# FFN weight low parts: an adding transfer on GpSimd's queue in place of a VectorE subtraction

## The chip, the cores and the metric

One core of one Trainium2 chip. The metric is the device time of one execution in microseconds (us). The kernel before takes 1315.03 us, the median of three runs (1314.34 to 1315.76). About 0.2% (2.6 us) is what a measurement of this kernel can tell from no change.

## The reference

A two-layer trunk on 512 tokens of width 1024, in float32. Layer 0 is a gated linear recurrence (HGRN2) and a SwiGLU FFN; then one shared K/V is projected; layer 1 is band attention and a second FFN. Every sub-layer has an RMSNorm, a shift and scale from a conditioning vector, and a gate on the residual. What the change touches are weights of the two FFNs:

```python
def swiglu(u, w_in, w_out):                     # w_in 1024 x 5632, w_out 2816 x 1024
    gate, up = jnp.split(u @ w_in, 2, axis=-1)
    return (jax.nn.silu(gate) * up) @ w_out
...
u = modulate(rms_norm(h, norm_ffn[layer]), sh2, sc2)
h = h + g2[:, None, :] * swiglu(u, ffn_w_in[layer], ffn_w_out[layer])
```

## The kernel before, in words

Activations lie as [features, tokens]: 8 tiles `h[j]` of 128 x 512. Every weight matrix comes in chunks of 128 x (8 x 128) float32 (512 KB; the third chunk of each FFN output tile has 6 blocks, 384 KB). `weight_plan` lists all chunks in the order in which TensorE uses them.

A float32 product is made of three products in the faster type float32r: value = high part + low part, and w x u is taken as high x high, high x low and low x high (`mm3`, L161, L162, L163; L163 is the one that uses a weight's low part). So each chunk is split (`split`): ScalarE copies the raw chunk into `wh`, rounded to float32r (L115), and VectorE subtracts, `wl = raw - wh` (L116). A chunk gives 24 products of 512 columns (18 in a third chunk).

`raw`, `wh` and `wl` each have three buffers (pool `wp`, bufs=3). So chunk i+3 can be split when TensorE has left chunk i. SyncE's queue (SP) issues the loads, and a raw buffer is free once both halves of the split have read it.

The program is recorded through a scheduler, which sets the order in each engine's queue by its own estimate of when things are ready; each engine then runs its queue strictly in order.

An FFN (`ffn`) has two parts. In the first, 22 pairs (gate, up) of output tiles, chunks `f1_n_0` and `f1_n_1` for layer 1, each from the eight normalised inputs `u3h/u3l`. Then `f1_s` (silu, ScalarE), `f1_at` (product, VectorE) and a split of that into `a{n}h/l`. In the second part, eight output tiles `f1_o_n` of three chunks each. The last tile of layer 1 is taken in two halves of the tokens (256 columns each), so it uses its three chunks twice.

Before layer 1's FFN stand the attention's output tiles `bo_0` to `bo_7`. Then `early_pair` takes the first pair, `f1_0_0` and `f1_0_1`, product by product in turn from inputs without the norm (`us3`; on TensorE `e_f`), while the norm is worked out: the mean square on TensorE (`n_ss`), `n_ms` on ScalarE, a power on GpSimd (`n3_rs`, L222), a broadcast by TensorE (`n_rb`). After it `modulated` makes `u3` tile by tile: `u_t` (VectorE), `u3h` (ScalarE), `u3l` (VectorE).

The names in the profile leave out numbers: `f` is any first-part chunk's output, `f_h` and `f_l` its weight parts, `r_f` the raw chunk; `f_o`, `f_o_h`, `f_o_l`, `r_f_o` the same of the second part; `mw` and `mrow` are rows of the modulation weights.

Of the kernel before, what the change touches and what calls it, by code (L numbers as in the profile page):

```python
# [43 lines left out]
# the last output tile is worked out in two parts of the tokens  # L44
# [18 lines left out]
def trunk(ctx: ExitStack, tc: tile.TileContext, d, out):  # L63
# [11 lines left out]
    # ---------------------------------------------------------------- constants, small operands  # L75
# [16 lines left out]
    # lower bound of the forget gates: softmax over the layers, cumulated, less the first  # L92
# [18 lines left out]
    # ---------------------------------------------------------------- helpers  # L111
    def split(raw, nk, n, nm, tag):
        wh = wp.tile([P, nk, n], F32R, tag=tag + "h", name=f"{nm}_h")
        wl = wp.tile([P, nk, n], F32R, tag=tag + "l", name=f"{nm}_l")
        A.activation(wh, raw, AF.Copy)  # L115
        V.tensor_sub(wl, raw, wh)  # L116
# [57 lines left out]
    def proj_tok(key, u, res):  # L174
        # token-major: out[token, 512 columns] for the four token blocks
        pss = [bank("_".join(str(x) for x in key) + f"_{b}") for b in range(NB)]
        for kp in range(KT // 2):
            wh, wl = weight(key + (kp,))
            for k2 in range(2):
                kt = 2 * kp + k2  # L180
                uh, ul = u[kt]
                for b in range(NB):
                    c = slice(b * P, (b + 1) * P)
                    T.matmul(pss[b], uh[:, c], wh[:, k2, :], start=kt == 0, stop=False)  # L184
                    T.matmul(pss[b], uh[:, c], wl[:, k2, :], start=False, stop=False)  # L185
                    T.matmul(pss[b], ul[:, c], wh[:, k2, :], start=False, stop=kt == KT - 1)  # L186
                    if kt == KT - 1 and b == NB - 1:
                        res += pss
                    yield

    def usplit(pool, tag, src, nm):
        # src (f32, SBUF) into its two float32r parts
        uh = pool.tile([P, S], F32R, tag=tag + "h", name=nm + "h")
        ul = pool.tile([P, S], F32R, tag=tag + "l", name=nm + "l")
        A.activation(uh, src, AF.Copy)
        V.tensor_sub(ul, src, uh)
        return uh, ul
# [18 lines left out]
    def rstd(pst, nm, b0=0, b1=NB):  # L216
        # 1/sqrt(mean + eps), tokens on partitions
        n = b1 - b0
        ms = sm.tile([P, NB], F32, tag="ms", name=f"{nm}_ms{b0}")
        A.activation(ms[:, 0:n], pst[:, b0:b1], AF.Identity, bias=eps)  # L220
        rs = sm.tile([P, NB], F32, tag="rs", name=f"{nm}_rs{b0}")
        G.tensor_tensor(rs[:, 0:n], ms[:, 0:n], nhalf[:, 0:n], op=ALU.pow)  # L222
# [63 lines left out]
    def mod_vector(i, bcol, mc):  # L286
        # 1024 entries of c_act @ mod_w, as [128, 8] columns, with the bias
# [61 lines left out]
    # ---------------------------------------------------------------- layer 0: first norm, modulation  # L349
# [8 lines left out]
    # the first six projections take the first inputs without their shifts, which come as a bias at the end  # L358
# [5 lines left out]
    def load_mod(j, v):  # L364
        # rows of the transposed modulation weights; v = 0: shift, 1: scale
# [117 lines left out]
    def core(p, qq, ks, f):  # L483
        # a yield stands where the tensor engine would wait
# [5 lines left out]
        def totals(hh, t):  # L490
            # products over blocks of hh -> over blocks of 2 hh
# [220 lines left out]
    with tc.manual_schedule():  # L712
# [142 lines left out]
    # ---------------------------------------------------------------- layer 0: FFN  # L855
# [17 lines left out]
    # ---------------------------------------------------------------- shared K/V, band attention  # L873
# [3 lines left out]
    with tc.tile_pool(name="attn", bufs=1) as ap:  # L877
# [67 lines left out]
        def transposes(hd, i, s):  # L945
            # block b of the keys goes to columns 384 b + 128 i
# [40 lines left out]
        def bfiller():  # L987
            # yields the pair whose buffers come next, or None
# [45 lines left out]
        for n in range(KT):  # L1034
# [14 lines left out]
    u = [modulated(up, "u", j, rb, a_f1[:, j:j + 1], mod["sh2b"][:, j:j + 1], "u3") for j in range(KT)]  # L1049
# [35 lines left out]
def weight_plan(d):  # L1085
# [7 lines left out]
    def ffn(layer):  # L1093
        nm = f"f{layer}"
        for n in range(FT):
            for v in range(2):
                one((nm, n, v), d["ffn_in"][layer, n, v])
        for n in range(KT):
            for ci, (k0, nk) in enumerate(((0, 8), (8, 8), (16, 6))):
                one((nm, "o", n, ci), d["ffn_out"][layer, n, :, k0:k0 + nk, :], nk)  # L1100
# [30 lines left out]
def _blocks(w, nk=None):  # L1131
    # [K, N] -> [N/128, 128 (k in tile), K/128, 128 (n in block)]
# [4 lines left out]
def _halves(w):  # L1137
    # [K, N] -> [N/512, K/256, 128, 2, 512]
# [8 lines left out]
def _layout(i):  # L1147
# [3 lines left out]
    # layer 0: sh1, sc1, g1, sc2, sh2, g2  # L1151
# [55 lines left out]
```

## Time and profile before

| | |
|---|---|
| median of three runs | 1315.03 us |
| span of the profiled execution | 1315.6 us |
| TensorE (PE) busy | 1292.7 us, 98% |
| VectorE (DVE) busy | 787.8 us, 60% |
| ScalarE (ACT) busy | 508.8 us, 39% |
| GpSimd (POOL) busy | 17.2 us, 24 instructions |
| loads on SP's queue | 174.08 MB |

The page gives the span as the profiled execution's only time. Times in rows are from the start of the span. PE is matmul, PEld the load of its stationary operand (here the weights), SPq the issue of transfers. In a row of the timeline stand the start, the duration, the engine, the line and the tiles; "x2" puts two like instructions together; the bracket tells how long the engine had been idle and what ended it.

### The profile page before, as it was taken

To read this page: it belongs to the slowest core of one execution; us is meant where nothing else is said; L and a number is where in the kernel's file an instruction comes from. 1 tells how busy PE (TensorE), PEld (TensorE's weight loads), DVE (VectorE), ACT (ScalarE), POOL (GpSimd) and SP (SyncE) were. 2 spreads that over 40 slices of the span, in tenths; PEclk is the share of its full clock that TensorE was granted. 3 is DMA by queue.
4 is the path that set the end of the run, shared out by engine and by line. 5 is a ranking of instruction groups with operands and counts; after the bars stand their busy time and mean duration, and the time that the engine had idled before them with its cause. 6 is when DMAs were issued, how large, how long until landed. Compare 5 with 4: busy or idle time off the path is not lost.

```text
span 1315.6 us, 18237 instructions
## 1 busy us (share of the span) xinstructions
PE 1292.7 (98%) x7248; PEld 1035.6 (79%) x7248; DVE 787.8 (60%) x1414; ACT 508.8 (39%) x838; POOL 17.2 (1%) x24
## 2 busy tenths in 40 slices
PE   8999999999999999999999999999999999999997
PEld 6888788888888877888888766667888888888886
DVE  7997865567876777633369567676753333332324
ACT  4454546444422222222237455664442222222220
POOL 0000000000000000000000000000000000000000
PEclk9999999999999999999999999999999999999998
DMA  9556732132788888632333322211233333333331
GB/s 363 169 166 202 217 97 71 57 95 68 243 276 266 257 272 280 192 100 88 104 111 96 96 87 66 77 56 62 67 112 97 96 97 96 96 92 100 88 89 64
DMA packets 52741, 175.24 MB, mean 133 GB/s; under 512 B 5936, under 2 KB 9392, under 8 KB 52656
## 3 DMA queue, kind: packets, MB, share of 16 engines
q1 hardware_dynamic: 52656, 174.08, 42.5%
q8 instruction: 57, 0.93, 0.3%
q14 instruction: 28, 0.23, 0.0%
HBM read 171.96 MB, written 2.10 MB: 132 GB/s over the span
## 4 chain that ended last, share of the span: by engine, by line
PE 80%; DMA 12%; DVE 4%; issue 3%; ACT 0%; SPq 0%; POOL 0%; DVEq 0%; POOLq 0%; ACTq 0%
DMA mw<-in_modw 11%; PE f L163 7%; PE f L161 7%; PE f L162 7%; PE f_o L161 6%; PE f_o L163 6%; PE f_o L162 6%; PE t L951 2%; PE s L934 2%; PE bo L965 1%; DVE mw L293 1%; PE bq L161 1%; PE bv L184 1%; PE bv L186 1%; PE bv L185 1%
## 5 line engine op out<-in xcount | busy, mean ns | idle before, releaser
L115 ACT ACTIVATE f_h<-r_f 128x1024 fp32r<-128x1024 f32 x88 | 92.9, 1058 | 194.5 <-PE f L162 89.7
L293 DVE SCALAR_TENSOR_TENSOR mw<-mw,crow 128x1024 f32<-128x1024 f32 x96 | 117.5, 1224 | 63.8 <-DMA mw<-in_modw 63.4
L116 DVE TENSOR_TENSOR f_l<-r_f,f_h 128x1024 fp32r<-128x1024 f32 x88 | 107.4, 1222 | 69.7 <-ACT f_h L115 69.4
L163 PE MATMUL f<-u1h,f_l 128*128 128x512 f32 x336 | 131.4, 392 | 2.9 <-DVE f_l L116 2.9
L161 PE MATMUL f<-u3h,f_h 128*128 128x512 f32 x336 | 132.2, 394 | 0.0
L163 PE MATMUL f<-u3h,f_l 128*128 128x512 f32 x336 | 131.6, 392 | 0.5 <-DVE f_l L116 0.5
L162 PE MATMUL f<-u1l,f_h 128*128 128x512 f32 x336 | 131.8, 393 | 0.0
L161 PE MATMUL f<-u1h,f_h 128*128 128x512 f32 x336 | 131.5, 392 | 0.0
L162 PE MATMUL f<-u3l,f_h 128*128 128x512 f32 x336 | 130.1, 388 | 0.0
L116 DVE TENSOR_TENSOR f_o_l<-r_f_o,f_o_h 128x1024 fp32r<-128x1024 f32 (+1 forms) x48 | 54.4, 1134 | 117.5 <-ACT f_o_h L115 117.5
L115 ACT ACTIVATE f_o_h<-r_f_o 128x1024 fp32r<-128x1024 f32 (+1 forms) x48 | 47.6, 991 | 173.7 <-PE f_o L162 131.1
L163 PEld LDWEIGHTS f<-u1h,f_l 128*128 128x128 f32 x336 | 63.1, 188 | 19.6 <-DVE f_l L116 5.8
L163 PEld LDWEIGHTS f<-u3h,f_l 128*128 128x128 f32 x336 | 63.1, 188 | 15.4 <-DVE f_l L116 0.8
L161 PEld LDWEIGHTS f<-u1h,f_h 128*128 128x128 f32 x336 | 63.1, 188 | 14.2 <-ACT u1h L282 0.3
L162 PEld LDWEIGHTS f<-u3l,f_h 128*128 128x128 f32 x336 | 63.1, 188 | 14.2
L162 PEld LDWEIGHTS f<-u1l,f_h 128*128 128x128 f32 x336 | 63.1, 188 | 13.2
L161 PEld LDWEIGHTS f<-u3h,f_h 128*128 128x128 f32 x336 | 63.2, 188 | 12.8 <-ACT u3h L282 0.3
L328 DVE TENSOR_TENSOR f_at<-f,f_s 128x512 f32<-128x512 f32 x42 | 28.9, 689 | 72.1 <-PE f L163 72.1
L940 ACT ACTIVATE sb<-sb,st 128x128 f32<-128x128 f32 (+1 forms) x64 | 35.7, 557 | 41.5 <-DVE st L939 41.4
L937 DVE CUSTOM_DVE_ANT_0 sb<-s,wb 128x128 f32<-128x128 f32 (+1 forms) x64 | 31.1, 490 | 29.9 <-PE s L934 29.6
L951 PE MATMUL t<-ident,sb 128*128 128x128 f32 x160 | 31.4, 294 | 0.0
L161 PE MATMUL bq<-uqh,bq_h 128*128 128x512 f32 x64 | 27.2, 427 | 0.0
(507 smaller groups left out, 2868.5 us busy)
## 6 DMA issues: line engine op xcount, KB each, us to landing
mw<-in_modw SPq DMA_DIRECT2D x96, 512.0 KB, 4.4
r_f<-in_ffn_in SPq DMA_DIRECT2D x88, 512.0 KB, 3.7
r_f_o<-in_ffn_out SPq DMA_DIRECT2D x32, 512.0 KB, 3.5
mrow<-in_modw SPq DMA_DIRECT2D x16, 512.0 KB, 9.0
r_f_o<-in_ffn_out SPq DMA_DIRECT2D x16, 384.0 KB, 3.1
r_av<-in_a_v SPq DMA_DIRECT2D x8, 512.0 KB, 3.8
r_g<-in_a_g SPq DMA_DIRECT2D x8, 512.0 KB, 3.7
r_ao<-in_a_out SPq DMA_DIRECT2D x8, 512.0 KB, 3.6
```

The source lines that it names most:

```text
L115: A.activation(wh, raw, AF.Copy)
L116: V.tensor_sub(wl, raw, wh)
L161: T.matmul(ps, wh[:, kt, :], uh, start=start, stop=False)
L162: T.matmul(ps, wh[:, kt, :], ul, start=False, stop=False)
L163: T.matmul(ps, wl[:, kt, :], uh, start=False, stop=stop)
L184: T.matmul(pss[b], uh[:, c], wh[:, k2, :], start=kt == 0, stop=False)
L293: V.scalar_tensor_tensor(mw, mw, 1.0, crow, op0=ALU.mult, op1=ALU.mult, accum_out=raw[:, j:j + 1])
L328: V.tensor_mul(at, res[1], sg)
L934: T.matmul(ps[:, 0:n], tq[r, c], kl[r, 0:n], start=False, stop=True)
L937: V.tensor_tensor_reduce(s[:, 0:n], ps[:, 0:n], wb[hd % NWB][:, S - n:S], scale=1.0, scalar=-3e38, op0=ALU.add, op1=ALU.max, accum_out=st[ ...
L940: A.activation(s[:, 0:n], s[:, 0:n], AF.Exp, bias=st[:, 1:2], accum_out=st[:, 2:3])
L951: T.transpose(tp[:, b * P:(b + 1) * P], s[:, b * P:(b + 1) * P], ident)
```

## The change

For layer 1's FFN (44 chunks of the first part, 24 of the second) and for the second part of layer 0's FFN (24 chunks), 92 in all, `split` no longer subtracts on VectorE. ScalarE writes the negated, rounded raw chunk into `wl`, and a transfer issued from GpSimd's queue adds the raw chunk to it in SBUF. Two numbers change with it: those chunks are recorded to be split 2 ahead (1 before) and loaded 3 ahead (2 before). Beside this, one small Silu activation after the fourth attention output tile makes ScalarE load its Silu table there. The other code that the edit adds (`take`, `fast_inputs`, `fast_tiles`) is reached only for layers in `FAST`, which is empty.

```diff
+FAST = ()
...
+    def by_dma(nm):
+        return nm.startswith(("f1", "f0_o"))
...
     def split(raw, nk, n, nm, tag):
         wh = wp.tile([P, nk, n], F32R, tag=tag + "h", name=f"{nm}_h")
-        wl = wp.tile([P, nk, n], F32R, tag=tag + "l", name=f"{nm}_l")
+        if not by_dma(nm):
+            wl = wp.tile([P, nk, n], F32R, tag=tag + "l", name=f"{nm}_l")
         A.activation(wh, raw, AF.Copy)
+        if by_dma(nm):
+            wl = wp.tile([P, nk, n], F32R, tag=tag + "l", name=f"{nm}_l")
+            A.activation(wl, raw, AF.Copy, scale=-1.0)
+            G.dma_start(out=wl, in_=raw, accum_op=ALU.add)
+            return wh, wl
         V.tensor_sub(wl, raw, wh)
         return wh, wl
...
     def fetch(i, ahead):
-        load(i + LOAD_AHEAD + 1)
+        load(i + (LOAD_AHEAD if not by_dma("_".join(str(x) for x in plan[i][0])) else 3) + 1)
...
-    def weight(key, ahead=SPLIT_AHEAD):
+    def weight(key, ahead=None):
+        if ahead is None:
+            ahead = 2 if by_dma("_".join(str(x) for x in key)) else SPLIT_AHEAD
...
             us.append(scaled(n, a_f1[:, n:n + 1], "us3"))
+            if n == 3:
+                with tc.issue_after(state["scaled"].ins):
+                    A.activation(csig[:, 0:1], cols[:, 0:1], AF.Silu)
```

In the new kernel the three products stand at L186, L187 and L188, the copy into `wh` at L125, the negation at L128 and the adding transfer at L129. SP's queue has the same loads in the same order. TensorE's queue differs only just after the early pair. There it stood, from the ninth product after that pair:

```order
L161 MATMUL f1_2_0_8495<-u3h0_8359,f1_2_0_h_8452 128x512
L162 MATMUL f1_2_0_8495<-u3l0_8360,f1_2_0_h_8452 128x512
L161 MATMUL f1_1_0_8425<-u3h2_8371,f1_1_0_h_8272 128x512
L163 MATMUL f1_1_1_8456<-u3h0_8359,f1_1_1_l_8422 128x512
L161 MATMUL f1_1_1_8456<-u3h1_8365,f1_1_1_h_8421 128x512
L162 MATMUL f1_1_1_8456<-u3l1_8366,f1_1_1_h_8421 128x512
```

and now, from the ninth as well:

```order
L186 MATMUL f1_2_0_8533<-u3h0_8394,f1_2_0_h_8456 128x512
L187 MATMUL f1_2_0_8533<-u3l0_8395,f1_2_0_h_8456 128x512
L186 MATMUL f1_1_0_8461<-u3h2_8406,f1_1_0_h_8299 128x512
L187 MATMUL f1_1_0_8461<-u3l2_8407,f1_1_0_h_8299 128x512
L188 MATMUL f1_1_0_8461<-u3h2_8406,f1_1_0_l_8301 128x512
L186 MATMUL f1_1_0_8461<-u3h3_8412,f1_1_0_h_8299 128x512
L187 MATMUL f1_1_0_8461<-u3l3_8413,f1_1_0_h_8299 128x512
L188 MATMUL f1_1_0_8461<-u3h3_8412,f1_1_0_l_8301 128x512
L188 MATMUL f1_1_1_8493<-u3h0_8394,f1_1_1_l_8308 128x512
L186 MATMUL f1_1_1_8493<-u3h1_8400,f1_1_1_h_8306 128x512
```

The first product with the low part of `f1_1_1` moved from 12th to 17th place. Further on, the last product with the high part of `f1_1_0` is now the 41st, and the first with the low part of `f1_2_1` the 75th, as before.

ScalarE's queue at the early pair and just after it, before:

```order
L115 ACTIVATE f1_0_1_h_8257<-r_f1_0_1_8207 128x1024
L205 ACTIVATE n3_sq6_0_8200<-h6_77 128x512
L242 ACTIVATE us3h6_8203<-h6_77,a_f1_8005 128x512
L115 ACTIVATE f1_1_0_h_8272<-r_f1_1_0_8255 128x1024
L242 ACTIVATE us3h7_8251<-h7_78,a_f1_8005 128x512
...
L115 ACTIVATE f1_1_1_h_8421<-r_f1_1_1_8270 128x1024
L115 ACTIVATE f1_2_0_h_8452<-r_f1_2_0_8419 128x1024
L282 ACTIVATE u3h2_8371<-u3_t2_8369,mod_sh2b_133 128x512
...
L318 ACT_TABLE_LOAD
L318 ACTIVATE f1_s0_8409<-n3_z0_8352,n3_bias_8348 128x512
```

and now:

```order
L125 ACTIVATE f1_0_1_h_8285<-r_f1_0_1_8232 128x1024
L128 ACTIVATE f1_0_1_l_8287<-r_f1_0_1_8232 128x1024
L230 ACTIVATE n3_sq6_0_8225<-h6_77 128x512
...
L125 ACTIVATE f1_1_1_h_8306<-r_f1_1_1_8283 128x1024
L128 ACTIVATE f1_1_1_l_8308<-r_f1_1_1_8283 128x1024
L125 ACTIVATE f1_2_0_h_8456<-r_f1_2_0_8304 128x1024
L307 ACTIVATE u3h2_8406<-u3_t2_8404,mod_sh2b_133 128x512
...
L125 ACTIVATE f1_2_1_h_8488<-r_f1_2_1_8454 128x1024
L220 ACTIVATE f1_a0h_8448<-f1_at0_8445 128x512
L128 ACTIVATE f1_2_1_l_8490<-r_f1_2_1_8454 128x1024
```

A negation (L128) follows each copy, mostly at once, ahead of what stood behind the copy; the table load has left the place ahead of `f1_s0`. On GpSimd's queue, which had nothing in the FFNs but the powers of the norms, the 92 transfers stand in the chunks' order; around layer 1's norm:

```order
L129 DMA f1_0_0_l_8236<-r_f1_0_0_8193 128x1024
L129 DMA f1_0_1_l_8287<-r_f1_0_1_8232 128x1024
L129 DMA f1_1_0_l_8301<-r_f1_1_0_8281 128x1024
L247 TENSOR_TENSOR n3_rs0_8350<-n3_ms0_8348,nhalf_93 128x4
L129 DMA f1_1_1_l_8308<-r_f1_1_1_8283 128x1024
```

The power `n3_rs` thus has three transfers of weights ahead of it. VectorE's queue has lost the 92 subtractions and is otherwise nearly as it was.

More of the change, by code (lines that the diff above doesn't have):

```diff
@@ L135, in fetch @@
     def fetch(i, ahead):
-        load(i + LOAD_AHEAD + 1)
-        while state["split"] < min(i + ahead + 1, len(plan)):
+        load(i + (LOAD_AHEAD if not by_dma("_".join(str(x) for x in plan[i][0])) else 3) + 1)
+        while state["split"] < min(i + ahead + 1, len(plan)) and plan[state["split"]][0][-1] not in ("c1", "c2"):
             key, _, nk, n = plan[state["split"]]
@@ L156, in weight, with take @@
         return ready.pop(key)
+    def take(key):
+        assert plan[state["used"]][0] == key, (plan[state["used"]][0], key)
+        load(state["used"] + LOAD_AHEAD + 1)
+        state["used"] += 1
+        state["split"] = state["used"]
+        return raws.pop(key)
     def mm3(ps, w, kt, u, start, stop):
@@ L309, in ffn, with slot, activated, kept @@
     def ffn(layer, z0, u, g2, side, finish):
         nm = f"f{layer}"
+        fast = layer in FAST
         with tc.tile_pool(name=nm, bufs=1) as fp:
             a = []
-            for n in range(FT):
+            raw_a = {}
+            if fast:
+                his, los, sums = fast_inputs(fp, *u, nm)
+                def slot(j, s):
+                    return his[j][:, s, :], los[j][s // 2][:, s % 2, :]
+                u = [(his[k // 2][:, 2 * (k % 2):2 * (k % 2) + 2, :].rearrange("p a c -> p (a c)"),
+                      los[k // 2][k % 2].rearrange("p a c -> p (a c)")) for k in range(KT)]
+            def activated(n):
+                if not fast or n < SPLIT_NOW:
+                    return sm.tile([P, S], F32, tag="sq", name=f"{nm}_at{n}", bufs=2)
+                g, e = divmod(n - SPLIT_NOW, 2)
+                if e == 0:
+                    raw_a[g] = fp.tile([P, 2, S], F32, tag=f"ab{g}", name=f"{nm}_ar{g}")
+                return raw_a[g][:, e, :]
+            def kept(n, at):
+                a.append(usplit(fp, f"a{n}", at, f"{nm}_a{n}") if not fast or n < SPLIT_NOW else at)
+            for n in range(PLAIN if fast else FT):
@@ L328, in ffn, with parts @@
                     V.tensor_mul(at, res[1], sg)
-                a.append(usplit(fp, f"a{n}", at, f"{nm}_a{n}"))
-            for n in range(KT):
-                chunks = ((0, 8), (8, 8), (16, 6))
+                kept(n, at)
+                if fast and n:
+                    for j in range(2 * n - 2, 2 * n):
+                        sums(j)
+            if fast:
+                fast_tiles(fp, nm, slot, activated, kept, side)
+            room = [(f"uo{j}", 2) for j in range(4)] + [("x1", 1), ("x2", 1)] + [(f"ab{g}", 1) for g in range(9)]
+            places = []
+            def parts(k):
+                if isinstance(a[k], tuple):
+                    return a[k]
+                if not places:
+                    tag, m = room.pop(0)
+                    t = fp.tile([P, 2 * m, S], F32R, tag=tag, name=f"{nm}_p{k}")
+                    places.extend((t[:, 2 * i, :], t[:, 2 * i + 1, :]) for i in range(m))
+                ah, al = places.pop(0)
+                A.activation(ah, a[k], AF.Copy)
+                V.tensor_sub(al, a[k], ah)
+                a[k] = ah, al
+                return a[k]
+            chunks = ((0, 8), (8, 8), (16, 6))
+            if fast:
+                pss = [bank(f"{nm}_o{n}_0") for n in range(2)]
+                for ci, (k0, nk) in enumerate(chunks):
+                    ws = [weight((nm, "o", n, ci)) for n in range(2)]
+                    for kt in range(nk):
+                        k = k0 + kt
+                        if k + 1 < FT:
+                            parts(k), parts(k + 1)
+                        for w, ps in zip(ws, pss):
+                            mm3(ps, w, kt, a[k], k == 0, k == FT - 1)
+                    next(side, None)
+                    next(side, None)
+                for n, ps in enumerate(pss):
+                    residual(n, ps, g2)
+                    later = finish(n, slice(0, S))
+            for n in range(2 if fast else 0, KT):
                 ws = []
@@ L1045, in trunk @@
             us.append(scaled(n, a_f1[:, n:n + 1], "us3"))
+            if n == 3:
+                with tc.issue_after(state["scaled"].ins):
+                    A.activation(csig[:, 0:1], cols[:, 0:1], AF.Silu)
         z0, rb = early_pair((("f1", 0, 0), ("f1", 0, 1)), us, acc, "n3")
-    u = [modulated(up, "u", j, rb, a_f1[:, j:j + 1], mod["sh2b"][:, j:j + 1], "u3") for j in range(KT)]
+    if 1 in FAST:
+        u = rb, a_f1, mod["sh2b"]
+    else:
+        u = [modulated(up, "u", j, rb, a_f1[:, j:j + 1], mod["sh2b"][:, j:j + 1], "u3") for j in range(KT)]
     acc = sm.tile([P, S], F32, tag="nacc", name="acc4", bufs=1)
@@ L1096, in ffn @@
             for v in range(2):
[L1097 to L1100, printed above, removed]
+                key = ("c1", "c2")[v] if layer in FAST and n >= PLAIN else v
+                one((nm, n, key), d["ffn_in"][layer, n, v])
+        chunks = tuple(enumerate(((0, 8), (8, 8), (16, 6))))
+        first = 2 if layer in FAST else 0
+        order = [(n, c) for c in chunks for n in range(first)] + [(n, c) for n in range(first, KT) for c in chunks]
+        for n, (ci, (k0, nk)) in order:
+            one((nm, "o", n, ci), d["ffn_out"][layer, n, :, k0:k0 + nk, :], nk)
     tok(("av", 0), d["a_v"][0])
@@ L1167, in _layout @@
     fi = np.stack([_blocks(w).reshape(2, FT, P, KT, P).transpose(1, 0, 2, 3, 4) for w in a["ffn_w_in"]])
+    for layer in FAST:
+        b = fi[layer, PLAIN:].copy()
+        for v, parts in enumerate((((0, 0), (0, 1)), ((1, 1), (1, 0)))):
+            fi[layer, PLAIN:, v] = np.concatenate([b[:, c, :, k::2, :] for c, k in parts], axis=2)
     r["ffn_in"] = np.ascontiguousarray(fi)
```

113 lines of the change are left out of this document (111 added, 2 removed).

## The prediction

> **What bounds the kernel now.** I read the page first (which engine is full), then the busy time by stretch: layer 0's first FFN part, which stays, and the three parts that change, then what TensorE waits for, and last the timeline at the places where a weight's low part is needed soonest.
>
> ```profile
> span 1315.6 us, 18237 instructions
> PE 1292.7 (98%) x7248; PEld 1035.6 (79%) x7248; DVE 787.8 (60%) x1414; ACT 508.8 (39%) x838; POOL 17.2 (1%) x24
> ```
>
> ```profile
> 320.00:520.00 200.00, 197.12 (x855) 159.46 (x854) 148.59 (x221) 58.93 (x77) 0.00 (x0) 1.00 0.79 256
> 556.10:673.00 116.90, 116.90 (x513) 95.90 (x512) 45.45 (x61) 32.17 (x39) 0.00 (x0) 1.00 0.32 96
> 960.00:1180.00 220.00, 220.00 (x962) 180.49 (x962) 78.57 (x85) 67.42 (x86) 0.00 (x0) 1.00 0.33 96
> 1181.00:1287.00 106.00, 106.00 (x465) 86.97 (x464) 32.07 (x34) 25.25 (x28) 0.00 (x0) 1.00 0.30 87
> ```
>
> Columns of the second fence: stretch, length, busy PE, PEld, DVE, ACT, POOL, granted clock, share of the 16 transfer engines, GB/s. The last three stretches are layer 0's second part and layer 1's two parts. TensorE is busy in all of each, at clock 1.00; VectorE is busy 30 to 39% and the transfer engines are a third used. So VectorE has nothing to give there: what its subtraction costs must be read from TensorE's waits for it.
>
> ```profile
> PE f L163 <- DVE f_l L116: 3.4, 7, 0.8
> L163 PE MATMUL f<-u3h,f_l 128*128 128x512 f32 x336 | 131.6, 392 | 0.5 <-DVE f_l L116 0.5
> L116 DVE TENSOR_TENSOR f_l<-r_f,f_h 128x1024 fp32r<-128x1024 f32 x88 | 107.4, 1222 | 69.7 <-ACT f_h L115 69.4
> L116 DVE TENSOR_TENSOR f_o_l<-r_f_o,f_o_h 128x1024 fp32r<-128x1024 f32 (+1 forms) x48 | 54.4, 1134 | 117.5 <-ACT f_o_h L115 117.5
> ```
>
> Of 3.4 us of such waits in the program, 0.5 us belong to layer 1 (`u3h`); the others are in layer 0's first part, which keeps its subtraction. The change takes 44 x 1.22 + 48 x 1.13 = 108 us of work off VectorE, and the path is shorter by half a microsecond at most, plus what stands still around it (below, 0.8).
>
> **The steady state.** Chunks follow each other like this:
>
> ```profile
> 1000.35 1.06 ACT L115 ACTIVATE f_h<-r_f 128x1024 fp32r<-128x1024 f32 x1 [3.88 <-PE f L162]
> 1001.45 1.23 DVE L116 TENSOR_TENSOR f_l<-r_f,f_h 128x1024 fp32r<-128x1024 f32 x1 [3.67 <-ACT f_h L115]
> 1002.70 22.30 SPq L132 DMA_DIRECT2D r_f<-in_ffn_in  x5
> 1005.85 1.06 ACT L115 ACTIVATE f_h<-r_f 128x1024 fp32r<-128x1024 f32 x1 [3.95 <-issue]
> 1268.15 1.06 ACT L115 ACTIVATE f_o_h<-r_f_o 128x1024 fp32r<-128x1024 f32 x1 [4.43 <-PE f_o L162]
> 1277.77 1.06 ACT L115 ACTIVATE f_o_h<-r_f_o 128x1024 fp32r<-128x1024 f32 x1 [3.89 <-PE f_o L162]
> ```
>
> The copy runs the moment TensorE leaves a buffer, that is at the start of chunk i for chunk i+2. A chunk lasts 5.50 us (1000.35 to 1005.85), so a product is issued each 5.50/24 = 0.229 us. The low part has two chunks' time. Added now: one negation (ScalarE, 1.06 us, same shape as the copy, so copy and negation end 2.0 us after the copy's start) and the transfer. Call L the time from the end of the negation until TensorE may load the low part. There is room for L = 11.0 + 0.2 - 2.0 = 9.2 us in the first part. In the second, two chunks are at least 9.6 us (1268.15 to 1277.77 are a third and a first chunk), which leaves 7.8.
>
> ScalarE has the time: it is idle 3.9 us before each copy. The raw buffer comes free later, when the transfer has read it. SP issued the next load at 1002.70, at the end of the subtraction; now it goes at 1002.4 + L, lands 3.7 us later, and is needed three chunks after 1000.35, at 1016.9. With L = 6 it lands at 1012.1, so 4.8 us remain. Behind that load on SP's queue stand only later loads (in layer 0 a few modulation rows too, whose vectors are needed much later).
>
> **What is L?** No adding transfer and no transfer from GpSimd is in the trace. The nearest rows:
>
> ```profile
> r_f<-in_ffn_in SPq DMA_DIRECT2D x88, 512.0 KB, 3.7
> r_f_o<-in_ffn_out SPq DMA_DIRECT2D x32, 512.0 KB, 3.5
> mrow<-in_modw SPq DMA_DIRECT2D x16, 512.0 KB, 9.0
> r_f_o<-in_ffn_out SPq DMA_DIRECT2D x16, 384.0 KB, 3.1
> 942.12 1.01 POOL L222 TENSOR_TENSOR n_rs<-n_ms,nhalf 128x4 f32<-128x4 f32 x1 [258.62 <-ACT n_ms L220]
> ```
>
> A plain load of the same size needs 3.7 us: the lower end. The same size behind a full queue at the start needs 9.0: the upper end. Between them I build 6.0: the plain 3.7, a second read of 512 KB (the engines' share, 0.33 x 5.50 = 1.8 us), and 0.5 us for the issue on GpSimd, half of its smallest row here. It is nearest to the loads' rows, since in these stretches the queues are as empty as there. For 384 KB I take 5.2, twice the 0.4 us by which its row is shorter. In the steady state 6.0 is inside 7.8 and 9.2, and the engines' time per chunk, 1.8 for the load and 3.6 for the addition, is 5.4 of 5.5. That is hidden, narrowly.
>
> The Trainium skill, "DMA: Bandwidth & Descriptors", section on the anatomy of one DMA on the SWDGE (GpSimd) path, fits a transfer as 2.0 us plus bytes/436e3; "Collectives: The Full Stack", section on the bandwidth ceiling, says the in-line add costs nothing of itself but needs two source reads, so half the rate. An estimate from both is L = 2.0 + 2 x 1.2 = 4.4 us, and by it the sum below would be 1.1 us instead of 6.8. No run here shows either page's figure yet.
>
> **The joints.** Where two chunks leave their buffers nearly together, or a chunk is used sooner, there is less room. Four places.
>
> ```profile
> 931.14 1.06 ACT L115 ACTIVATE f_h<-r_f 128x1024 fp32r<-128x1024 f32 x1 [2.67 <-PE bo L162]
> 937.58 0.19 PEld L163 LDWEIGHTS e_f<-us3h,f_l 128*128 128x128 f32 x1
> 936.63 1.06 ACT L115 ACTIVATE f_h<-r_f 128x1024 fp32r<-128x1024 f32 x1 [3.17 <-PE bo L162]
> 948.77 2.01 ACT L115 ACTIVATE f_h<-r_f 128x1024 fp32r<-128x1024 f32 x2 [0.36 <-PE e_f L162]
> 951.47 1.38 ACT L282 ACTIVATE u3h<-u_t,mod_sh2b 128x512 fp32r<-128x512 f32 x2 [0.69 <-DVE u_t L279]
> 949.85 0.47 PE L161 MATMUL f<-u3h,f_h 128*128 128x512 f32 x1
> 952.25 0.50 PE L161 MATMUL f<-u3h,f_h 128*128 128x512 f32 x1
> 953.29 0.50 PE L163 MATMUL f<-u3h,f_l 128*128 128x512 f32 x1 [0.53 <-DVE f_l L116]
> ```
>
> 1. The early pair uses `f1_0_1` from its sixth product on, not a chunk later. Its copy starts at 931.14, the negation ends at 933.15, the low part is loaded at 937.58: room 4.4. With L = 6.0 TensorE waits 1.6 us.
>
> 2. `f1_1_1` is copied only when the early pair ends (948.77). The two copies in that row take 2.01; now copy and negation do: 950.8. Its low part stands 17th after 949.85: 949.85 + 16 x 0.229, less 0.23 because weights are loaded a product ahead, is 953.3. Room 2.5, wait 3.5. Before, TensorE lost 1.04 - 0.23 = 0.8 here (952.25 to 953.29), and that goes, so 2.7. With the negation ahead of it, `u3h2` starts at 948.77 + 3.1 = 951.9 instead of 951.47; that half microsecond lies inside the wait.
>
> ```profile
> 960.52 1.28 ACT L318 ACT_TABLE_LOAD   x1
> 962.92 1.05 ACT L115 ACTIVATE f_h<-r_f 128x1024 fp32r<-128x1024 f32 x1
> 963.87 0.62 ACT L195 ACTIVATE f_a0h<-f_at 128x512 fp32r<-128x512 f32 x1
> ```
>
> 3. `f1_2_1` gets the buffer of `f1_1_0` after the 41st product and is needed at the 75th: 34 x 0.229 - 0.23 = 7.55 us. In it: 0.3 until the copy starts, copy 1.05, `f_a0h` 0.62, negation 1.06 (the table load, 1.28, has gone from here; TensorE never waited for it). Room 4.5, wait 1.5. After these waits the chunks stand apart again and the steady room holds.
>
> ```profile
> 1283.26 1.06 ACT L115 ACTIVATE f_o_h<-r_f_o 128x1024 fp32r<-128x1024 f32 x1 [4.43 <-PE f_o L162]
> 1287.33 0.85 ACT L115 ACTIVATE f_o_h<-r_f_o 128x768 fp32r<-128x768 f32 x1 [3.01 <-PE f_o L162]
> 1290.31 0.19 PEld L163 LDWEIGHTS f_o<-f_a8h,f_o_l 128*128 128x128 f32 x1
> 1293.13 0.19 PEld L163 LDWEIGHTS f_o<-f_a16h,f_o_l 128*128 128x128 f32 x1
> ```
>
> 4. In the last tile's first half the products are half as long. The second chunk: 1283.26 + 2.0 to 1290.31, room 5.0, wait 1.0. The third: 1287.33 + 1.7 to 1293.13 + 1.0, room 5.1 against 5.2, 0.1 more.
>
> GpSimd's power `n_rs` at 942.12 stands behind the transfer of `f1_1_0`, whose negation ends at 936.63 + 2.0, so it has 3.5 us for that issue: nothing. Layer 0's second part begins from a steady state: nothing.
>
> Sum: 1.6 + 2.7 + 1.5 + 1.0 = 6.8 us. The span, 1315.6, is 0.6 above the median of 1315.03 and within the runs shown, so I put the sum on the median: **1321.8 us**, 0.5% slower. At L = 3.7 only the second place counts (1.2 - 0.8), 1315.4. At L = 9.0: 4.6 + 5.7 + 4.5 + 4.0, and 1.2 for each of 15 tiles of the second parts, 37 us, 1352.
>
> **The rivals.**
>
> *The transfer is quick, not slower.* Below L = 4.9 the four waits come to under 2.6 us, which no measurement tells from none. For it: the plain load's 3.7, and the estimate of 4.4 by the page (1316.1). Against it: the second read and the issue must then cost little over 1 us together. Time 1314.5 to 1317.6. Chance 0.28.
>
> *The transfer engines become the bound.* The load's 1.8 us leave 3.7 of each 5.5 us chunk. If the addition costs three times a load's share instead of twice (two reads and a write one after the other, 5.4), a chunk takes 7.2: 44 x 1.7 in the first part, and in the second, where a load is 0.30 x 5.0 = 1.5, four times 1.5 make 6.0 of the 15.1 / 3 = 5.03 there (1268.15 to 1283.26 is a tile of three), 48 x 1.0; 123 us in all, 1438. It decides from an addition over 3.7 us of all 16 engines, or L over 7.8. For it: two reads already fill 5.4 of 5.5. Against it: in layer 0's first part the engines moved 256 GB/s at a share of 0.79, 324 at full share against 96/0.33 = 291 here, so a byte costs less when there is more to move. Chance 0.22.
>
> *VectorE's relief shows.* The 0.5 and 0.8 us of waits go, and nothing comes in their place: 1314.2, still inside 0.2%. To be faster than that TensorE's own pace would have to change, and with VectorE 74% busy it was 197.12/855 = 0.231 us a product, with VectorE 36% busy 220/962 = 0.229. Chance of over 0.2% faster: 0.04.
>
> **How the numbers follow.** Joints late and steady state hidden, L from 4.9 to 8: chance 0.46, 1317.6 to 1330, and 1321.8 its middle. Quick: 0.28, same. Engines bound: 0.22. Faster 0.04. Same is 0.27 (the quick case less its edge), slower 0.69. The range reaches down to 1314.2 (nothing waits, the gain of 0.8) and up to 1350 (L at its upper end); outside lie most of the bound case and half of the faster one, 0.2.
>
> **What would show it.** Right: in the steady stretches TensorE still busy 100% and a share of the transfer engines of 0.6 to 0.95 (0.33 before); L read from negation to landing about 6 us; TensorE waits for transfers of `f_l` near the early pair, some microseconds each, and about 1 us near the end; VectorE's busy time down by 108 us, ScalarE's up by about 94 us. Wrong: waits for `f_l` or for raw chunks in every chunk (the engines are the bound), or none at all (quick). The forecast falls most easily on L, since each microsecond of it is worth about 4 us.

## The result: 0.3% slower, and the profile after

The changed kernel takes 1318.34 us, the median of five runs (1316.97 to 1320.36), against 1315.03 (1314.16 to 1316.03) for five of before on the same chip: ratio 1.0031, 95% interval 1.0018 to 1.0043 (the two medians alone give 1.0025). Forecast were 1321.8 us, slower, for waits at four joints. The direction and the kind of loss came out; of the 6.8 us about half did.

The profiled execution of after is the lowest of the five (1316.97), and its span, 1315.1, is even shorter than that of before. So the span doesn't show the loss; the stages do. This table is made from the first and last starts of the matmul groups of each tile, in us:

| | before | after |
|---|---|---|
| start to layer 0's FFN | 320.3 | 318.6 |
| its first part (subtraction kept) | 235.9 | 234.4 |
| its second part to layer 1's early pair | 380.5 | 380.7 |
| early pair (place 1) | 13.2 | 14.6 |
| layer 1's first part (places 2, 3) | 231.5 | 232.9 |
| second part up to the last half tile (place 4) | 113.7 | 113.8 |
| last half tile and the final norm's matmuls | 13.5 | 13.1 |

The two stages that the change leaves alone differ by 3.2 us between these two executions, and layer 0's first part lay between 232.7 and 236.4 in all the kernels below that leave it alone. That hides a loss of this size in any single span. The later stages repeat within some tenths, and there the loss is 1.4 + 1.4 = 2.8 us. The 0.4 us of the last row is not the change's: the half tile's products take 9.1 us in both, and the final norm's last four matmuls (`n_rb`) 1.2 us before and 0.7 after, but 1.2 again in e4, e7 and e8 below. First the page of after: the engines, and the transfers' queues (packets, MB, share of 16 engines).

```profile
span 1315.1 us, 18452 instructions
PE 1291.8 (98%) x7248; PEld 1034.1 (79%) x7248; DVE 684.9 (52%) x1322; ACT 589.5 (45%) x931; POOL 96.9 (7%) x116
q1 hardware_dynamic: 52656, 174.08, 41.7%
q0 software_dynamic: 13248, 46.14, 19.6%
...
r_f<-in_ffn_in SPq DMA_DIRECT2D x88, 512.0 KB, 4.6
f_l<-r_f POOLq DMA_DIRECT2D x44, 512.0 KB, 5.6
r_f_o<-in_ffn_out SPq DMA_DIRECT2D x32, 512.0 KB, 4.3
```

VectorE has 103 us less to do, ScalarE 81 more, and TensorE is as busy as before. The additions are the new second queue; they land 5.6 us after their issue, and the loads beside them have become slower. The 88 `r_f` loads of the page mix two stages: those of layer 0's first part have no additions beside them and stayed at 4.7 us (320 to 550 us). Layer 1's alone (925 to 1182 us), before and after:

```profile
r_f<-in_ffn_in SPq DMA_DIRECT2D x41, 512.0 KB, 3.5
r_f<-in_ffn_in SPq DMA_DIRECT2D x41, 512.0 KB, 4.9
```

The second parts' loads (`r_f_o`) went from 3.5 to 4.3. Now the three changed stretches, with the same columns as before: busy PE, PEld, DVE, ACT, POOL, granted clock, the transfer engines' share, GB/s.

```profile
556.10:673.00 116.90, 116.90 (x512) 95.73 (x511) 21.67 (x38) 49.31 (x58) 18.26 (x21) 1.00 0.83 189
960.00:1180.00 220.00, 220.00 (x962) 180.35 (x961) 28.38 (x41) 103.29 (x124) 35.26 (x41) 1.00 0.86 190
1181.00:1287.00 106.00, 106.00 (x465) 86.97 (x464) 9.36 (x13) 42.83 (x49) 18.05 (x21) 1.00 0.83 189
```

The engines' share went from 0.33 to 0.86 in layer 1's first part, and TensorE still has no gap: the steady state hides the addition. An addition costs (0.86 - 0.33) x 5.50 = 2.9 us of all engines, where 3.6 were assumed. TensorE's products wait for transfers twice in the whole program:

```profile
PE e_f L188 <- DMA f_l<-r_f: 1.2, 1, 1.2
PE f L188 <- DMA f_l<-r_f: 1.1, 1, 1.1
PE f L187 <- DVE u3l L308: 0.3, 1, 0.3
```

They are places 1 and 2. The third row is what place 2 does to VectorE's vectors, whose ScalarE half now stands behind a negation. The timeline there (`L128` is the negation, `L129` the issue of the adding transfer, `L188` the product with the low part):

```profile
930.46 0.86 POOL L129 DMA_DIRECT2D f_l<-r_f  x1 [4.52 <-ACT f_l L128]
936.15 0.19 PEld L188 LDWEIGHTS e_f<-us3h,f_l 128*128 128x128 f32 x1 [1.59 <-DMA f_l<-r_f]
...
948.19 1.04 ACT L128 ACTIVATE f_l<-r_f 128x1024 fp32r<-128x1024 f32 x1
949.14 1.05 ACT L125 ACTIVATE f_h<-r_f 128x1024 fp32r<-128x1024 f32 x1
949.54 0.92 POOL L129 DMA_DIRECT2D f_l<-r_f  x1 [7.92 <-ACT f_l L128]
950.85 0.50 PE L186 MATMUL f<-u3h,f_h 128*128 128x512 f32 x1
951.64 0.50 PE L187 MATMUL f<-u3l,f_h 128*128 128x512 f32 x1 [0.29 <-DVE u3l L308]
952.66 0.40 PE L188 MATMUL f<-u3h,f_l 128*128 128x512 f32 x1
954.15 0.51 PE L188 MATMUL f<-u3h,f_l 128*128 128x512 f32 x1 [1.09 <-DMA f_l<-r_f]
954.49 0.40 PE L186 MATMUL f<-u3h,f_h 128*128 128x512 f32 x1
...
967.56 0.19 PEld L188 LDWEIGHTS f<-u3h,f_l 128*128 128x128 f32 x1 [0.27 <-DMA f_l<-r_f]
```

At place 1 the negation ended at 930.2 and the weights are loaded at 936.15: L = 6.0, as forecast. At place 2 it ended at 949.23, and the product starts at 954.15: L = 4.9. There TensorE loses 0.79 - 0.23 and 1.49 - 0.23, 1.8 us in all, where it lost 0.8 before. The product behind a wait also comes 0.34 us later and not 0.23, so counting starts is safer: against an even pace of 0.229 us the first 24 products after the early pair lose 2.3 us, and lost 1.0 before. Place 2 thus costs 1.3 us. The last row is place 3: the weight load waits 0.27 us for the transfer, which costs TensorE 0.1 us. Together with the 1.4 of place 1 that is the whole 2.8 us of the two stages.

### The profile page after: what moved, and what is told of

It is laid out like the page before. It is cut to its first block, busy times and chain, and to the rows that moved or that the text cites. A ratio compares the mean times of both kernels' runs of the same rounds, so it can differ in the third digit from the quotient of the medians.

```text
span 1315.1 us, 18452 instructions
## 1 busy us (share of the span) xinstructions
PE 1291.8 (98%) x7248; PEld 1034.1 (79%) x7248; DVE 684.9 (52%) x1322; ACT 589.5 (45%) x931; POOL 96.9 (7%) x116
## 4 chain that ended last, share of the span: by engine, by line
PE 78%; DMA 11%; DVE 6%; issue 4%; ACT 1%; SPq 0%; POOL 0%; DVEq 0%; POOLq 0%; ACTq 0%
DMA mw<-in_modw 9%; PE f L188 7%; PE f L187 7%; PE f L186 7%; PE f_o L187 6%; PE f_o L188 6%; PE f_o L186 6%; PE t L1161 2%; PE s L1144 2%; PE bo L1175 1%; PE o L808 1%; DVE mw L318 1%; PE bq L186 1%; PE g L186 1%; PE bv L209 1%
## 5 line engine op out<-in xcount | busy, mean ns | idle before, releaser
L125 ACT ACTIVATE f_h<-r_f 128x1024 fp32r<-128x1024 f32 x88 | 92.9, 1057 | 164.8 <-PE f L187 85.1
L188 PE MATMUL f<-u1h,f_l 128*128 128x512 f32 x336 | 132.7, 395 | 1.9 <-DVE f_l L131 1.9
L187 PE MATMUL f<-u3l,f_h 128*128 128x512 f32 x336 | 132.4, 394 | 0.3 <-DVE u3l L308 0.3
L186 PE MATMUL f<-u3h,f_h 128*128 128x512 f32 x336 | 131.9, 393 | 0.0
L188 PE MATMUL f<-u3h,f_l 128*128 128x512 f32 x336 | 130.5, 389 | 1.1 <-DMA f_l<-r_f 1.1
L187 PE MATMUL f<-u1l,f_h 128*128 128x512 f32 x336 | 131.2, 391 | 0.0
L186 PE MATMUL f<-u1h,f_h 128*128 128x512 f32 x336 | 130.7, 390 | 0.0
L125 ACT ACTIVATE f_o_h<-r_f_o 128x1024 fp32r<-128x1024 f32 (+1 forms) x48 | 47.4, 988 | 137.1 <-PE f_o L187 78.4
L188 PEld LDWEIGHTS f<-u1h,f_l 128*128 128x128 f32 x336 | 63.1, 188 | 16.9 <-DVE f_l L131 4.2
L188 PEld LDWEIGHTS f<-u3h,f_l 128*128 128x128 f32 x336 | 63.1, 188 | 15.8 <-DMA f_l<-r_f 1.8
L186 PEld LDWEIGHTS f<-u3h,f_h 128*128 128x128 f32 x336 | 63.1, 188 | 15.1 <-ACT u3h L307 0.3
L187 PEld LDWEIGHTS f<-u1l,f_h 128*128 128x128 f32 x336 | 63.1, 188 | 14.7
L186 PEld LDWEIGHTS f<-u1h,f_h 128*128 128x128 f32 x336 | 63.1, 188 | 13.8 <-ACT u1h L307 0.3
L187 PEld LDWEIGHTS f<-u3l,f_h 128*128 128x128 f32 x336 | 63.2, 188 | 13.2 <-DVE u3l L308 0.6
L129 POOL DMA_DIRECT2D f_o_l<-r_f_o x48 | 41.7, 869 | 429.8 <-ACT f_o_l L128 419.4
L129 POOL DMA_DIRECT2D f_l<-r_f x44 | 38.0, 863 | 444.9 <-ACT f_l L128 439.6
L332 DVE SCALAR_TENSOR_TENSOR h<-f_o,mod_g2b,h 128x512 f32<-128x512 f32 (+1 forms) x9 | 6.2, 691 | 95.0 <-PE f_o L188 95.0
L131 DVE TENSOR_TENSOR f_l<-r_f,f_h 128x1024 fp32r<-128x1024 f32 x44 | 53.5, 1218 | 0.1
```

Of the source, the lines that this page charges most:

```text
L129: G.dma_start(out=wl, in_=raw, accum_op=ALU.add)
L186: T.matmul(ps, wh[:, kt, :], uh, start=start, stop=False)
L187: T.matmul(ps, wh[:, kt, :], ul, start=False, stop=False)
L188: T.matmul(ps, wl[:, kt, :], uh, start=False, stop=stop)
```

## The experiments

The theory (J): the loss is only the waits at the joints, set by L; the steady state is hidden as long as the shares of the transfer engines sum to less than one. Its rivals: the table load and the new numbers for splitting and loading ahead cost something by themselves; or the 92 transfers slow everything a little (loads, ports), joints or not. All ratios and their intervals are to runs of the kernel before on the same chip; its medians there were 1314.40 us for e1 to e4, 1312.74 for e5 to e7 and 1313.28 for e8 (a ratio is not just the quotient of two medians). Stages in us, as above:

| | early pair | layer 1, first part | ratio to before |
|---|---|---|---|
| before | 13.2 | 231.5 | |
| after | 14.6 | 232.9 | 1.0031 |
| e1_sub | 13.2 | 231.5 | 1.0001 |
| e2_joints_sub | 13.2 | 231.5 | 1.0010 |
| e3_only_joints | 13.7 | 232.4 | 1.0017 |
| e4_no_table | 15.0 | 232.9 | 1.0032 |
| e7_copy | 13.2 | 231.4 | 1.0005 |
| e8_first_sub | 14.2 | 232.9 | 1.0025 |

**e1_sub: VectorE subtracts again in all 92; the table load and the distances stay.**

```diff
-            A.activation(wl, raw, AF.Copy, scale=-1.0)
-            G.dma_start(out=wl, in_=raw, accum_op=ALU.add)
+            V.tensor_sub(wl, raw, wh)
```

> The changed kernel with the subtraction back on VectorE in all 92 chunks (no negation, no adding transfer); the table load's new place and the recording ahead stay. Theory J (the loss is two waits of TensorE for late low parts at the early pair and just after it): the loss goes, 1314 to 1315.5, and the adding transfers carry all of it. Rival S (the loss is in the order or the earlier splitting, not in the transfer): 1317 to 1319 as in the changed kernel. The table load alone should show nothing, under 1 us.

Measured: 1313.51 us, ratio 1.0001 (0.9984 to 1.0018). The loss is gone, in both stages too, so it belongs to the negations and transfers (e7 below tells these two apart); the two other edits are worth nothing that shows, which here means under some 0.2%.

**e4_no_table: the Silu activation after the fourth output tile taken out of the changed kernel.**

```diff
-            if n == 3:
-                with tc.issue_after(state["scaled"].ins):
-                    A.activation(csig[:, 0:1], cols[:, 0:1], AF.Silu)
```

> The changed kernel without the small Silu activation, so that the table is loaded again after the norm, where f1_s0 wants it. Theory J: the third joint (f1_2_1) has 1.3 us less room on ScalarE and shows or does not show a wait of up to 1 us: 1318 to 1319.5. If the table's move was itself worth something, 1319.5 or more; if it cost something, under 1317.5.

Measured: 1317.73 us, ratio 1.0032 (1.0018 to 1.0045), the same as with it, though 0.3 us under the range of theory J. Its waits at places 1 and 2 are 1.5 and 1.1; the wait at `f1_2_1` that theory J allowed for is not in its list.

**e2_joints_sub and e3_only_joints: the joints apart from the rest.** The first gives VectorE the six chunks `f1_0_*` to `f1_2_*` and leaves 86 transfers; the second leaves transfers only for `f1_0_1` and `f1_1_1`.

```diff
+            if not nm.startswith(("f1_0_", "f1_1_", "f1_2_")):   # e2;  e3: if nm in ("f1_0_1", "f1_1_1"):
                 A.activation(wl, raw, AF.Copy, scale=-1.0)
                 G.dma_start(out=wl, in_=raw, accum_op=ALU.add)
+            else:
+                V.tensor_sub(wl, raw, wh)
```

> The changed kernel with VectorE's subtraction for the six chunks f1_0_0 to f1_2_1 alone, and the adding transfer for the other 86. Theory J: no wait for a transfer is left, the time is that of the kernel before within 0.1% (1314 to 1316), and the 86 transfers stay hidden although the engines' share is above 0.8. Rival C (the cost is spread: 92 transfers, contention with the loads, or time outside the span): about 86/92 of the loss stays, 1317.5 to 1319.

> The converse: the adding transfer for f1_0_1 and f1_1_1 alone, VectorE for the other 90. Theory J: nearly the whole loss stays, 1.4 us at the early pair and about 1 us after it, 1317 to 1318.5. Rival C: 2/92 of the loss, 1315.

Measured: e2 1315.40 us, 1.0010 (0.9995 to 1.0026), no change that can be told, with both stages those of before. A loss spread over the 86 transfers is thus not in layer 1's first part; over the whole program the interval leaves room for up to 0.26%. But theory J expected no wait, and TensorE waited for one transfer, in layer 0's second part:

```profile
598.37 0.87 POOL L130 DMA_DIRECT2D f_o_l<-r_f_o  x1 [4.62 <-ACT f_o_l L129]
606.98 0.50 PE L191 MATMUL f_o<-f_a8h,f_o_l 128*128 128x512 f32 x1 [0.70 <-DMA f_o_l<-r_f_o]
```

From the negation's end, 0.3 us ahead of the issue, this is L = 8.9, over the room of 7.8 that was worked out for the second parts. In the changed kernel the same addition had 8.1 and just made it. So the steady state is hidden narrowly, and one late addition is enough to show; why this one was late is open. e3 1316.57 us, 1.0017 (1.0004 to 1.0030): two transfers alone bring back a part of the loss, under the 1317 to 1318.5 of theory J. TensorE's waits for them in e3:

```profile
PE f L191 <- DMA f_l<-r_f: 0.6, 1, 0.6
PE e_f L191 <- DMA f_l<-r_f: 0.2, 1, 0.2
```

So the loss sits where the theory puts it, but in the two stages it was only half as large, 1.4 us of 2.8. At place 1 the reason is L: `f1_0_1` landed in 4.7 us, in the changed kernel in 5.6. At place 2 it isn't: `f1_1_1` landed in 4.9 us there against 4.6, but TensorE's order is another one in e3 and needs that low part at the 20th product and not at the 17th. L is no constant: what does it depend on?

**e7_copy: the same transfer without the addition.** It copies the raw chunk over the negation.

```diff
-            G.dma_start(out=wl, in_=raw, accum_op=ALU.add)
+            G.dma_start(out=wl, in_=raw)
```

> Question: what are the 5.6 us from issue to landing made of? The same transfer, same queue and size, but without the addition (it copies the raw chunk over the negation: one read of 512 KB fewer; the low part is then the raw chunk). Theory A (the second read takes its time on the engines, about half of the addition's 2.9 us): the transfer engines' share in layer 1's first part falls from 0.86 to about 0.6, the landing from 5.6 to about 4.1 us, the loads come back from 4.6 towards 4.0, TensorE's waits for transfers of f_l (2.3 us in sum) fall under 0.8, and the time is 1314.5 to 1316.5. Theory B (the landing is mostly the fixed cost of a transfer issued by GpSimd): landing over 5.0, waits over 1.8 us, time 1317 to 1319.

Measured: 1314.41 us, ratio 1.0005 (0.9991 to 1.0019), and TensorE waits for no transfer at all. The landings (the loads from 925 to 1182 us, as above) and layer 1's first part:

```profile
r_f<-in_ffn_in SPq DMA_DIRECT2D x41, 512.0 KB, 3.5
f_l<-r_f POOLq DMA_DIRECT2D x44, 512.0 KB, 2.9
...
960.00:1180.00 220.00, 220.00 (x963) 180.53 (x962) 28.38 (x41) 102.13 (x123) 21.72 (x41) 1.00 0.58 194
```

Theory A holds, by more than it said: landing 2.9 instead of 4.1, and the loads are back at the 3.5 us of before. The negation and the issue are still there, so the loss is the addition's. A copy takes 0.58 - 0.33 = 0.25 of a chunk's time on the engines, the addition 0.53, 2.1 times as much; the same number of bytes is written, 190 and 194 GB/s. Its issue keeps GpSimd 0.53 us instead of 0.86. So of the 5.6 us to landing, 2.7 go with the addition.

**e8_first_sub: only `f1_0_0` back to VectorE**, so that the load that takes its raw buffer is through before `f1_0_1` is added.

```diff
+            if nm != "f1_0_0":
                 A.activation(wl, raw, AF.Copy, scale=-1.0)
                 G.dma_start(out=wl, in_=raw, accum_op=ALU.add)
+            else:
+                V.tensor_sub(wl, raw, wh)
```

> Question: why did the adding transfer land in 5.6 us at the early pair and in 4.5 to 4.6 at the other joints? Only f1_0_0 goes back to VectorE's subtraction, so its raw buffer is free some 4 us sooner and the load that takes it is through before f1_0_1's transfer is issued; nothing else changes. Theory A (a transfer alone lands in 4.5 to 4.8 us, with a load in flight beside it in 5 to 7): f1_0_1 lands in 4.5 to 4.8, TensorE's wait in the early pair falls from 1.2 to 0.1 to 0.4 and the pair from 14.6 to 13.3 to 13.7 us; the first FFN part of layer 1 stays at 232.6 to 233.1 with its wait of about 1.1; time about 1 us under the changed kernel's, ratio to before 1.0020 to 1.0028. Theory B (the first transfers of a stage are slow by themselves, whatever runs beside them): f1_0_1, now the first one, lands in 5.6 or more, the wait stays over 1.0 and the pair at 14.4 to 14.8.

Measured: 1317.10 us, ratio 1.0025 (1.0013 to 1.0037). `f1_0_1` landed after 5.2 us, the wait in the early pair fell from 1.2 to 0.7, the pair to 14.2; place 2 stayed. That lies between the theories. The window of that transfer:

```profile
931.75:936.95 5.20, 4.53 (x20) 3.38 (x18) 3.08 (x5) 2.85 (x5) 0.92 (x1) 1.00 0.54 102
```

The neighbour is gone (share 0.54, where after has 0.81 during this transfer, below), and about a third of the stage's loss with it. That it is now the stage's first transfer is not what makes the rest: in the changed kernel the first one of the stage is `f1_0_0`, and it landed in 4.7 us; in e3 `f1_0_1` is the first of the whole program, and it landed in 4.7 too. Besides its own packets the transfer queues show one single packet of an instruction queue (q14) during e8's addition, as at place 1 below, and none in e3. Whether that costs the half microsecond was not tested, so the rest is open.

The changed kernel itself says more. Here are five of its 44 first-part additions, each row the time from issue to landing: the first (`f1_0_0`), place 1, place 2, place 3, and one of the next. Below them the other queues' packets during place 1's.

```profile
925.01:929.71 4.70, 4.70 (x22) 3.87 (x21) 2.81 (x6) 2.40 (x4) 0.93 (x1) 1.00 0.60 115
930.46:936.06 5.60, 4.53 (x20) 3.38 (x18) 3.48 (x5) 3.25 (x5) 0.98 (x2) 1.00 0.81 189
949.54:954.14 4.60, 3.23 (x12) 1.67 (x10) 4.19 (x7) 4.02 (x6) 1.77 (x2) 1.00 0.63 120
963.03:967.53 4.50, 4.50 (x21) 3.52 (x19) 1.38 (x2) 3.06 (x5) 1.72 (x2) 1.00 0.69 131
969.37:975.87 6.50, 6.50 (x30) 5.35 (x29) 1.25 (x2) 2.72 (x4) 1.68 (x2) 1.00 1.01 245
...
q1 hardware_dynamic: 144, 0.52, 33.2%
q14 instruction: 1, 0.01, 0.4%
```

Of the 44, the three during which the engines were less than 0.7 busy landed in 4.5 to 4.7 us; the other 41 took 5.1 to 7.4. The packets say it more sharply. A whole load (q1, 144 packets) ran during place 1's addition. Of all 92 additions of the changed kernel five had no packet of a load during them: the first, those of places 2 and 3, and the two of place 4. The four of 512 KB among them landed in 4.5 to 4.7 us, all others of this size in 4.8 or more. With a load beside it an addition is slower, and places 2 to 4 had none. This is how they lie in one kernel; the run made to test it, e8, gave a third.

**e5_f0_too: the adding transfer in layer 0's first part too**, where the engines are at 0.79 without it.

```diff
-        return nm.startswith(("f1", "f0_o"))
+        return nm.startswith(("f1", "f0"))
```

> Question: what do the 16 transfer engines do where they are already busy? Here the 44 chunks of layer 0's first part, where their share was 0.79, get their low parts by the adding transfer as well. Theory A (shares add up and the engines are the bound once the sum passes 1; an addition costs 0.53 of a 5.5 us chunk, 2.9 us): 0.8 x 235 + 44 x 2.9 = 316 us of engine time for a stage that lasted 235; some 20 of it can slip into the second part, so the first part becomes 290 to 315 us and the program 1375 to 1400 us, with TensorE waiting for raw chunks or low parts in nearly every chunk there. Theory B (busy engines move more per unit of time, the additions squeeze in; only joints cost): first part under 242 us, program 1318 to 1326.

Measured: 1394.31 us, ratio 1.0623 (1.0590 to 1.0656). The first part lasts 305.9 us, inside the 290 to 315 of theory A. TensorE's products wait 19 times for a transfer of `f_l`, 52.9 us in all; one of these waits (1.1) is place 2, so 18 of the 44 chunks of this stage are waited for, and not nearly every one as theory A had it.

```profile
330.00:600.00 270.00, 220.45 (x874) 173.62 (x874) 111.76 (x191) 91.56 (x111) 31.03 (x36) 0.93 0.94 272
```

**e6_double: two additions to each low part, one after the other.**

```diff
-            A.activation(wl, raw, AF.Copy, scale=-1.0)
+            A.activation(wl, raw, AF.Copy, scale=-2.0)
             G.dma_start(out=wl, in_=raw, accum_op=ALU.add)
+            G.dma_start(out=wl, in_=raw, accum_op=ALU.add)
```

> Question: where does the steady state stop hiding the transfer? Each low part gets two additions one after the other (the negation by -2, so that the low part comes out doubled). Theory A (L has room 9.2 us in the first part and 7.8 in the second, engines have room for one addition only): the second addition starts when the first has landed, L becomes 0.3 + 5.6 + 0.9 + 5.6 = 12.4 or more, a chunk needs (12.4 + 1.8)/2 = 7.1 us instead of 5.5 and 5.03; 44 x 1.6 + 48 x 2.1 = 170 us, by the engines (1.8 + 2 x 2.9 = 7.6 a chunk) up to 200: 1480 to 1520 us, TensorE waiting for f_l and f_o_l in nearly every chunk. Theory B (the second addition, on warm data and with its descriptors overlapped, adds under 3.5 us to L): the steady state stays hidden, only the joints grow by 3 us each: 1322 to 1335.

Measured: 1531.15 us, ratio 1.1653 (1.1626 to 1.1680), 11 us above the upper end of theory A. The waits, and layer 1's first part:

```profile
PE f_o L189 <- DMA f_o_l<-r_f_o: 74.0, 41, 3.6
PE f L189 <- DMA f_l<-r_f: 62.9, 39, 3.6
...
1099.26 0.86 POOL L130 DMA_DIRECT2D f_l<-r_f  x1 [5.96 <-DMA f_l<-r_f]
1106.96 0.86 POOL L130 DMA_DIRECT2D f_l<-r_f  x1 [5.95 <-DMA f_l<-r_f]
...
1050.00:1250.00 200.00, 158.94 (x609) 121.41 (x610) 18.00 (x26) 62.65 (x75) 44.21 (x51) 0.93 0.92 201
```

A chunk takes 7.70 us (1099.26 to 1106.96), against 1.8 + 2 x 2.9 = 7.6 by the engines' shares and 7.1 by L. Now TensorE waits in nearly every chunk, and the engines stand at 0.92 of their time. In both kernels, where the shares would sum to more than one, the mean time of a chunk grew. Which of the two limits binds in e6 this run does not separate, as they lie so close.

## Why the prediction was half right

**What held.** VectorE's 103 us bought nothing: TensorE is 100% busy in the steady stretches before and after, and before it waited for the subtraction only 0.5 us in layer 1. The steady state hides the transfer, narrowly, as e2 shows. The kind of loss is the forecast one, TensorE waiting for low parts after the early pair's chunks, and stage by stage e1, e2 and e7 leave nothing else. (The stages account for 2.8 us; the medians differ by 3.3, and the interval of 1.0018 to 1.0043 is 2.4 to 5.7 us, so 2.8 lies in it.)

**The joints, one by one.** The step that failed is one L, 6.0, for all four places.

| place | forecast, us | measured, us | L forecast | L measured |
|---|---|---|---|---|
| 1, early pair | 1.6 | 1.4 | 6.0 | 6.0 |
| 2, `f1_1_1` | 2.7 | 1.3 | 6.0 | 4.9 |
| 3, `f1_2_1` | 1.5 | 0.1 | 6.0 | 4.8 |
| 4, last tile, second and third chunk | 1.0 and 0.1 | no wait | 6.0 and 5.2 | 4.8 and 4.2 |

Measured L is issue to landing and the 0.3 us from the negation's end to the issue; place 1's loss is that of its stage. As the median of all, 5.6 + 0.3 = 5.9, the 6.0 was good. But the joints are not the median: at places 2 to 4 no load ran beside the addition. That fits with chunks that stand still there: the loads wait for raw buffers and so stand still too. The profile of before had a part of this in view. The stretches of the four places, in before:

```profile
930.00:936.00 6.00, 6.00 (x28) 4.90 (x27) 4.34 (x8) 2.31 (x3) 0.00 (x0) 1.00 0.53 151
949.00:954.00 5.00, 4.47 (x21) 3.23 (x20) 4.78 (x9) 3.16 (x4) 0.00 (x0) 1.00 0.00 0
964.00:969.00 5.00, 5.00 (x24) 4.09 (x23) 4.25 (x6) 3.51 (x5) 0.00 (x0) 1.00 0.38 115
1285.00:1290.00 5.00, 5.00 (x35) 4.55 (x34) 2.80 (x4) 1.48 (x2) 0.00 (x0) 1.00 0.00 0
```

No transfer at all moves at places 2 and 4, and place 1 is the busiest of the four, as its landing is the slowest. Place 3 does not follow: 0.38 in before, and yet its addition landed as soon as the others, as in the changed kernel no load ran during it. With L = 4.9 at places 2 to 4 the working on record gives 1.6 + (2.4 - 0.8) + 0.4 + 0 = 3.6 us, where the stages show 1.4 + 1.3 + 0.1 = 2.8. That 3.6 also comes near the 3.3 by which the medians differ is no proof of it. I had the mean share of the stage, 0.33, and put it everywhere.

**Place 3's other part.** Copy, `f_a0h` and negation were summed to 2.73 us; the copy started at 960.20 and the negation ended 2.5 us later. ScalarE's rows overlap: at place 2 the negation starts at 948.19 with a duration of 1.04 and the next copy at 949.14. Each of a run of activations takes 0.95, a tenth less than its row says. That is also why ScalarE's busy time rose by 81 us, though the rows of the negations (L128) come to 45.9 + 46.6 = 92.5, near the 94 of the forecast. It put 0.2 us more room at place 3, 4.7, which with L = 4.8 leaves the 0.1 us that was measured.

**How 6.0 was built.** The parts were 3.7 (a plain load), 1.8 (a second read) and 0.5 (the issue). A plain copy by this path lands in 2.9 (e7), the addition adds 2.7, of which 1.5 are time of the engines ((0.53 - 0.25) x 5.50) and 0.3 a longer issue (0.86 us, where 0.5 was assumed); the other 0.9 is not accounted for. The base was too high (the 3.7 itself mixed two stages, and in these stretches a load took 3.5), the addition too low: two errors of opposite sign, so that the median came out at 5.9 and place 1 at 6.0 is luck. The estimate of 4.4 from the Trainium skill, "DMA: Bandwidth & Descriptors", section on the anatomy of one DMA, with "Collectives: The Full Stack", section on the bandwidth ceiling, came close to the additions that ran alone (4.8 to 5.0 with the 0.3 us ahead of the issue), and the half rate, which that section measures for a collective, agrees with the 2.1 measured between e7's copies and the additions. It doesn't hold beside other transfers, where 5.1 to 7.4 us were measured to landing.

**The rivals.** "Quick" asked for L under 4.9, and places 2 to 4 had 4.9 or a little less; place 1 alone was slower, and the loss is therefore just above what can be told. "Engines the bound" fell, as an addition costs 2.9 of the engines' time and not over 3.7; e5 shows that the mechanism is real, and e6 that one more addition per chunk is too much, be it by the engines or by L. "VectorE's relief" did not show: e7, where VectorE is as free as in after and TensorE waits for no transfer, is no faster than before.

## What to carry to other kernels

Moving work off an engine that is 60% busy gave nothing, as the bottleneck didn't wait for it: read the row of waits for that engine first (here 0.5 us). The replacement with more latency cost at the joints, where chunks have less than a full period to be ready; size each joint by what the transfer engines do at that very place, not by the stage's mean. Test the steady state by summing their shares (0.33 + 0.53 held, sums past one made the mean chunk longer), and compare the slowest landing with the room too, not only the median: in e2 a single one of 8.6 us was enough for a wait. And where unchanged stages vary by more than the effect, compare stages and not spans.

## What was new about the hardware

- A transfer from GpSimd's queue within SBUF of 512 KB landed after 2.9 us as a copy (e7, the median of layer 1's first part) and after 4.5 to 7.4 us as an addition to its destination (the changed kernel, the same 44 chunks; 4.5 to 4.7 with no load beside it); an addition took 2.1 times the engines' time and kept GpSimd 0.86 us for its issue, a copy 0.53.
- Layer 1's loads (`r_f`) slowed beside additions from a median of 3.5 to 4.9 us; beside copies (e7) they stayed at 3.5.
- In the stretches where TensorE had gaps (82% busy in e5, 79% in e6) its granted clock was 0.93, while it was 1.00 in the same kernels' full stretches as in before. It was not the bound there, so no time is put down to it.
